# A hybrid encoder layer on one core: seven parts in the second feed-forward product, two stage-2 weight blocks prepared early, operand splits and loads re-timed

## The chip, the core and the metric

The kernel runs on one core of a Trainium2 chip. Its engines are TensorE (PE; its weight loads are shown as PEld), VectorE (DVE), ScalarE (ACT), GpSimd (POOL) and SyncE (SP), which issues nearly all DMAs. Each engine works through its own queue in order. The metric is the device time of one execution in microseconds; before the change it is 2453.44 us, the median of 3 runs (2451.5 to 2454.14).

## What is computed

One encoder layer on 2048 + 256 positions of width 1024, in float32, with a final norm:

```python
h = rmsnorm(x, norm1_g)
q, k, v, g, lr, u, vs, xp = split(h @ w_in)
a_out = gla_mixer(q, k, v, g, lr, ...)        # 512 channels, two directions, chunks of 64
b_out = spatial_gating(gelu(u), gelu(vs), ...) # 256 channels, chunks of 128
c_out = pool_mixer(xp, pool_w, pool_scale)     # 256 channels, windows 2, 4, 8, 16
x = x + concat([a_out, b_out, c_out]) @ w_o
h = rmsnorm(x, norm2_g)
a, up = split(h @ w1)                          # 2816 channels each
a = shift(a, -1) * cw[0] + a * cw[1] + shift(a, 1) * cw[2] + cb
x = x + (silu(a) * up) @ w2
y = rmsnorm(x, norm_f)
```

## The kernel before

Every large product works on float32 values split into a rounded high part and the rest: `split` copies the high part on ACT and subtracts it on DVE, or on POOL where it is told so. `mm3` then issues three matmuls (high times high, high times low, low times high). One such triple, followed by a call of `pipe.tick()`, is the unit of the schedule, a tick.

**How order is set.** TensorE's order is written out by hand. The other work stands in Python generators that are put into a `Pipe`, a heap of due ticks: `pipe.add(gen, d)` starts one d ticks from now, each `yield d` puts off its next piece by d ticks, and `tick()` emits what is due. An engine then runs its instructions in the order in which they were emitted, each waiting for its inputs and for its output buffer. From the second tile of stage 2 on, DVE, ACT, POOL and SP keep that order too; before it (stage 1 and the first tile of stage 2) a planner orders them.

**Stages.** Stage 1 runs 18 tiles of 128 positions through the first 1312 columns of `w_in` (weight tiles `wk0` to `wk7`) and computes the chunk sums of the gated attention in `post1`. Stage 2 runs the tiles again, in reverse order in five groups, through the other 1024 columns (`vk0` to `vk7`; raw blocks come through four `rawb` buffers, `w2prep` splits one). After each group `out2` does the product with `w_o`, adds `x`, and stores it in DRAM (`d_x`); `stat2` sums its squares with a matmul `pn`. The last group's `out2` runs at the start of the feed-forward part, with the operands of the first block being split beside it (`hprep`).

**Feed-forward.** Three blocks of two halves of 384 positions (halves 0 and 1). For each of 22 hidden columns `ffn1` computes both halves with seven half-depth products instead of eight, by sums of operands. The weight side (A11, S1, S2, S3, S4, A12, A22) is made by `operands()`, one operand per product, three products ahead (`astep` at the first triple of each). In block 0 it loads A22, A21, A11, A12 and makes S1 to S4 on POOL (`comb`), and `keep` stores them in DRAM for blocks 1 and 2. Raw operands share a ring of NR = 9 buffers; in blocks 1 and 2 they are loaded ND = 7 ahead. The activation side is eight arrays in four tiles: p = 0 holds B11 and B21, p = 1 holds T3 and B22, p = 2 holds T1 and T2, p = 3 holds T4. Their products come in the order B11, T1, T2, T3, B22, B21, T4. `bmake` makes these sums for the next block and stores them in DRAM; `bload` reads and splits them for the next block while the last part of this one runs (p = 0 and 2 on DVE, p = 1 and 3 on POOL), starting 30 ticks after the last hidden column begins, each piece 3 ticks after the one before.

A column has 28 ticks. `gate` then makes the gated hidden values, split into `uh` and `ul`. `ffn2` multiplies the columns of a part (`PARTS`) with the second weights, for eight output columns c and both halves, and adds the result into `x2`. One such c is a job: its raw weights come through `rg` (NRG = 3 buffers), `prepw2` splits them into `gh` and `gl` (2 buffers each), two jobs ahead of loads. One hidden column beyond the part is computed before the part's `ffn2` starts, except in the last part, where none is left: there the last column's values are the newest, and `late` puts them behind the others for the first c. In the last part `sqadd` also squares the new x on ACT and adds the squares into `acc` on POOL. `finish` turns them into the final norm: a matmul `pn`, a power on POOL, a matmul `pr`, eight multiplications on DVE, two stores, and then the loads of the next block's x (`load2f`). For half 0 of the last block `last_norm` does the same in another order.

## Time and profile before

| what | us |
|---|---|
| median of 3 runs | 2453.44 |
| the profiled execution | 2454.75 |
| its span | 2453.0 |
| stage 1 | about 0 to 372 |
| stage 2 and the product with `w_o` | about 372 to 840 |
| feed-forward block 0 | about 839 to 1382 |
| feed-forward block 1 | about 1382 to 1912 |
| feed-forward block 2 and the tail | about 1912 to 2453 |

The profile is one execution. Starts are counted from the start of its span. A row of the list of instructions gives the start, the time taken, engine, line, operation, output and inputs, and in brackets how long the engine stood idle before it and what released it. A row of waits gives the engine and the line that waited, what it waited for, the total, how often, and the longest. Matmuls are pipelined, so each takes about twice the distance to the next. The busy times of rows that are merged (x2, x4) run from the first start to the last end.

### The profile page before, as it was taken

To read this page: it belongs to the slowest core of one execution; us is meant where nothing else is said; L and a number is where in the kernel's file an instruction comes from. 1 tells how busy PE (TensorE), PEld (TensorE's weight loads), DVE (VectorE), ACT (ScalarE), POOL (GpSimd) and SP (SyncE) were. 2 spreads that over 40 slices of the span, in tenths; PEclk is the share of its full clock that TensorE was granted. 3 is DMA by queue.
4 is the path that set the end of the run, shared out by engine and by line. 5 is a ranking of instruction groups with operands and counts; after the bars stand their busy time and mean duration, and the time that the engine had idled before them with its cause. 6 is when DMAs were issued, how large, how long until landed. Compare 5 with 4: busy or idle time off the path is not lost.

```text
span 2453.0 us, 36854 instructions
## 1 busy us (share of the span) xinstructions
PE 2382.1 (97%) x13280; PEld 2268.6 (92%) x13280; DVE 1679.3 (68%) x2981; ACT 1034.4 (42%) x1928; POOL 794.2 (32%) x748
## 2 busy tenths in 40 slices
PE   8999998999999889999999899999999999999997
PEld 7899996988988789999999899999999999999997
DVE  6766657676666786777777686666677766666666
ACT  6444445333333443333334544433345533344334
POOL 3332221111011664455444622323223521222122
PEclk9999999999999999999999999999999999999998
DMA  6333224565664754454535464444434543333222
GB/s 202 136 129 112 78 73 150 173 191 149 205 191 128 221 164 128 136 171 155 159 104 160 142 223 118 145 134 126 127 102 155 181 138 100 103 112 104 92 94 87
DMA packets 227771, 343.51 MB, mean 140 GB/s; under 512 B 25634, under 2 KB 124962, under 8 KB 227588
## 3 DMA queue, kind: packets, MB, share of 16 engines
q1 hardware_dynamic: 220564, 318.21, 41.7%
q0 software_dynamic: 6752, 22.55, 2.4%
q8 instruction: 105, 1.72, 0.3%
q14 instruction: 78, 0.64, 0.1%
q10 hardware_dynamic: 272, 0.39, 0.0%
HBM read 261.81 MB, written 79.25 MB: 139 GB/s over the span
## 4 chain that ended last, share of the span: by engine, by line
PE 53%; DVE 4%; issue 3%; POOL 3%; DMA 1%; ACT 1%; SPq 0%; DVEq 0%; POOLq 0%; ACTq 0%
PE py L171 7%; PE py L170 6%; PE py L169 6%; PE fD L1158 3%; PE fA L1160 3%; PE fD L1159 3%; PE fA L1158 3%; PE fD L1160 3%; PE fA L1159 3%; PE fB L1158 2%; PE fB L1160 2%; PE fB L1159 2%; PE fC L1158 2%; PE fC L1160 2%; PE fC L1159 2%
## 5 line engine op out<-in xcount | busy, mean ns | idle before, releaser
L162 POOL TENSOR_TENSOR S<-S,S 128x512 fp32r<-128x512 f32 x242 | 329.7, 1363 | 757.5 <-ACT S L161 724.1
L171 PE MATMUL py<-uh,gl 128*128 128x384 f32 (+1 forms) x1056 | 359.2, 340 | 6.8 <-DVE gl L1225 6.7
L169 PE MATMUL py<-uh,gh 128*128 128x384 f32 (+1 forms) x1056 | 359.6, 341 | 3.2 <-ACT gh L1223 3.1
L170 PE MATMUL py<-ul,gh 128*128 128x384 f32 (+1 forms) x1056 | 358.9, 340 | 3.7 <-DVE ul L1188 3.7
L1270 DVE TENSOR_TENSOR x<-py,x 128x384 f32<-128x384 f32 (+1 forms) x384 | 213.1, 556 | 159.3 <-PE py L171 157.6
L162 DVE TENSOR_TENSOR A<-A,A 128x512 fp32r<-128x512 f32 x198 | 158.0, 798 | 178.5 <-ACT A L161 169.9
L161 ACT ACTIVATE A<-A 128x512 fp32r<-128x512 f32 x198 | 124.4, 630 | 218.8 <-issue 71.0
L171 PEld LDWEIGHTS py<-uh,gl 128*128 128x128 f32 x1056 | 200.1, 190 | 10.4 <-DVE gl L1225 10.4
L161 ACT ACTIVATE S<-S 128x512 fp32r<-128x512 f32 x242 | 152.2, 629 | 135.3 <-PE fE L1160 62.1
L170 PEld LDWEIGHTS py<-ul,gh 128*128 128x128 f32 x1056 | 200.1, 190 | 5.7 <-DVE ul L1188 5.3
L169 PEld LDWEIGHTS py<-uh,gh 128*128 128x128 f32 x1056 | 200.2, 190 | 4.8 <-ACT gh L1223 4.4
L1223 ACT ACTIVATE gh<-rg 128x384 fp32r<-128x384 f32 (+1 forms) x198 | 97.4, 493 | 223.8 <-PE py L170 207.0
L1158 PE MATMUL fA<-B,A 128*128 128x386 f32 (+1 forms) x528 | 180.2, 341 | 0.0
L1160 PE MATMUL fA<-B,A 128*128 128x386 f32 (+1 forms) x528 | 179.3, 339 | 0.0
L1159 PE MATMUL fA<-B,A 128*128 128x386 f32 (+1 forms) x528 | 178.6, 338 | 0.0
L169 PE MATMUL pm<-wk,xh 128*128 128x512 f32 (+2 forms) x432 | 166.4, 385 | 7.0 <-ACT wk L164 6.7
L170 PE MATMUL pm<-wk,xh 128*128 128x512 f32 (+2 forms) x432 | 157.0, 363 | 0.4 <-DVE wk L165 0.3
L171 PE MATMUL pm<-wk,xl 128*128 128x512 f32 (+2 forms) x432 | 156.2, 362 | 0.6 <-DVE xl L162 0.6
L1225 DVE TENSOR_TENSOR gl<-rg,gh 128x384 fp32r<-128x384 f32 (+1 forms) x198 | 119.4, 603 | 8.0 <-ACT gh L1223 8.0
L171 PE MATMUL pw<-mh,ol 128*128 128x512 f32 (+1 forms) x320 | 118.7, 371 | 2.9 <-DVE ol L162 2.9
L169 PE MATMUL qm<-vk,xh 128*128 128x512 f32 x288 | 118.9, 413 | 2.2 <-ACT vk L164 2.2
L169 PE MATMUL pw<-mh,oh 128*128 128x512 f32 (+1 forms) x320 | 118.4, 370 | 0.0
(279 smaller groups left out, 6223.2 us busy)
## 6 DMA issues: line engine op xcount, KB each, us to landing
A<-in_w SPq DMA_DIRECT2D x242, 256.0 KB, 3.7
S<-ds_S SPq DMA_DIRECT2D x176, 256.0 KB, 2.7
rg<-in_w SPq DMA_DIRECT2D x150, 192.0 KB, 2.7
xt<-in_xT SPq DMA_DIRECT2D x35, 512.0 KB, 4.3
ds_S<-S SPq DMA_DIRECT2D x66, 256.0 KB, 2.1
rawo<-dw SPq DMA_DIRECT2D x64, 256.0 KB, 4.4
dx<-xr SPq DMA_DIRECT2D x24, 256.0 KB, 2.5
rg<-in_w SPq DMA_DIRECT2D x48, 128.0 KB, 2.3
```

What stands on the lines that cost most here:

```text
L161: SC.activation(hi, src, AF.Copy)
L162: (eng or V).tensor_tensor(out=lo, in0=src, in1=hi.bitcast(F32), op=ALU.subtract)
L169: TE.matmul(out, lh, rhs_h, start=first, stop=False)
L170: TE.matmul(out, lh, rhs_l, start=False, stop=False)
L171: TE.matmul(out, ll, rhs_h, start=False, stop=last)
L1158: TE.matmul(o, ah, bh, start=st, stop=False, skip_group_check=True)
L1159: TE.matmul(o, ah, bl, start=False, stop=False, skip_group_check=True)
L1160: TE.matmul(o, al, bh, start=False, stop=kk == 3, skip_group_check=True)
L1223: SC.activation(gh[:, 0:n], rv, AF.Copy)
L1225: V.tensor_tensor(out=gl[:, 0:n], in0=rv, in1=gh[:, 0:n].bitcast(F32), op=ALU.subtract)
L1270: V.tensor_tensor(out=x2[:, c, 1:1 + no], in0=py[q][:, 0:no], in1=x2[:, c, 1:1 + no], op=ALU.add)
```

## The change

It makes these edits; the numbers in a schedule are ticks.

- `PARTS`: seven parts, six of three columns and one of four, instead of eight (five of three, two of two, one of three). `NU` becomes 4; `uh` and `ul` stay at 8 buffers (`NUT`).
- In the last part the jobs c = 0 and c = 1 are issued as one list (`late`): of c = 0 first the three older columns of half 1, then of half 0, then the newest column of half 1, all of c = 1 for half 1, the newest of half 0 for c = 0, and all of c = 1 for half 0. Job 2's weights are split at the end of c = 0, and job 4's are loaded at the end of the list.
- `bload` follows a table, `BORDER`: T1 and T2 (p = 2) at 13 to 22, within the last hidden column; p = 0 and p = 1 at 42 to 68; p = 3 at 78 to 90. Three loads are under way instead of four.
- `finish` starts 14 and 36 ticks after the last part instead of 2 and 28. The last norm's matmuls and diagonals come ahead of what is left of the other half's `finish` (`pipe.flush()` is moved), and all its diagonals are made on ACT.
- The first block's x is loaded from the schedule, 30 and 60 ticks after the feed-forward part begins (`first_x`), not at once. `stat2` of the last group comes 16 instead of 8 ticks after its products.
- `vk0` and `vk1` get a pool of their own (`vx`), allocated ahead of stage 1's weights; they are split during tiles 15 and 16, and their `rawb` buffers then load blocks 4 and 5. At the start of stage 2, blocks 2, 3 and 4 are split, and 5, 6 and 7 during its first three triples' worth of k.
- Rings: NR 9 to 8, ND 7 to 6, NRG 3 to 2, NZ 2 to 1 (stage 1's zeroed attention buffers). In `operands`, S3's sum is made one step earlier and the load of the next A11 goes out one step later, behind the store of S4. The load of `rg` for three jobs ahead is issued at a job's fifth triple instead of the third.

```diff
-NR = 9
-ND = 7
+NR = 8
+ND = 6
-NRG = 3
+NRG = 2
+NVX = 2
-HL = (1, 2)
+XG = 30
+BORDER = ((0, 2, 13), (1, 2, 16), (2, 2, 19), (3, 2, 22), (0, 0, 42), (0, 1, 45), (1, 0, 48), (1, 1, 52),
+          (2, 0, 56), (2, 1, 60), (3, 0, 64), (3, 1, 68), (0, 3, 78), (1, 3, 82), (2, 3, 86), (3, 3, 90))
-PARTS = (3, 3, 3, 3, 3, 2, 2, 3)
+PARTS = (3, 3, 3, 3, 3, 3, 4)
+NUT = 8
...
+    vx = pool("vx", 1)
+    vk = [vx.tile([P, 2, W2C], F32R, name=f"vk{k}") for k in range(NVX)]
+    def w2prep(k):
+        split(vk[k][:, 0], vk[k][:, 1], pre[k], vc[:, V_G1 + k:V_G1 + k + 1])
+        if k + NRAW < KD:
+            wbload(k + NRAW)
...
-        NZ = 2
+        NZ = 1
...
+            if NT - 1 - NVX <= i < NT - 1:
+                pipe.add(w2early(i - NT + 1 + NVX), 12)
...
-                        if g and k + 3 < KD:
-                            w2prep(k + 3)
+                        if g and k + NVX + 3 < KD:
+                            w2prep(k + NVX + 3)
...
-            pipe.add(stat2(u, acc, alloc), 8)
+            pipe.add(stat2(u, acc, alloc), 16 if between else 8)
...
-        for k in range(3):
+        for k in range(NVX, NVX + 3):
             w2prep(k)
-            if k == EV:
+            if k == NVX:
                 end1()
...
-            for p, _ in PAIRS:
-                load(0, p)
-            yield box["wait"]
-            for kk in range(4):
-                for p, eng in PAIRS:
...
+            for kk, p in todo[:NX - 1]:
+                load(kk, p)
+            at = 0
+            for n, (kk, p, tick) in enumerate(BORDER):
+                if tick > at:
+                    yield tick - at
+                    at = tick
+                m = 2 if p < 3 else 1
+                hi, src = B[p][:, 0, 0:m, kk, 0:w], got.pop((kk, p))
+                SC.activation(hi, src, AF.Copy)
+                yield 1
+                (GP if p % 2 else V).tensor_tensor(out=B[p][:, 1, 0:m, kk, 0:w], in0=src, in1=hi.bitcast(F32), op=ALU.subtract)
+                yield 1
+                at += 2
+                if n + NX - 1 < len(todo):
+                    load(*todo[n + NX - 1])
...
                 s2 = comb(rawt4("S2"), s1, a11, ALU.subtract)
+                s3 = comb(a21, a11, a21, ALU.subtract)
                 yield
                 operand(j, "S1", s1)
                 keep(j, "S1", s1)
-                s3 = comb(a21, a11, a21, ALU.subtract)
...
                 operand(j, "S4", s4)
-                if more:
-                    a11 = rawop(j + 1, "A11")
-                else:
+                if not more:
                     ahead(2)
                 yield
                 operand(j, "A12", a12)
                 keep(j, "S4", s4)
-                if not more:
+                if more:
+                    a11 = rawop(j + 1, "A11")
+                else:
                     ahead(2)
...
             if late:
-                order = [o for o in order if o[1] < n - 1] + [o for o in order if o[1] == n - 1]
+                a, b = range(n - 1), range(n)
+                order = [(t, q, k) for t, q, ks in ((0, 1, a), (0, 0, a), (0, 1, b[-1:]), (1, 1, b), (0, 0, b[-1:]), (1, 0, b))
+                         for k in ks]
...
+                if late:
+                    if (t, q, k) == (0, 0, n - 1):
+                        begin(prepw2(jobs[2]))
+                    if at == len(order) - 1:
+                        loadw2(jobs[4])
+                elif t and at == 0 and t + 1 < len(jobs):
                     begin(prepw2(jobs[t + 1]))
-                if at == 2 and 1 <= t and t + 3 < len(jobs):
+                elif t and at == min(4, len(order) - 1) and t + 3 < len(jobs):
                     loadw2(jobs[t + 3])
...
-                o, i, sc = dg[:, b * P:b * P + n], ident[:, P - n:P], r[:, b:b + 1]
-                if b % 2:
-                    SC.activation(o, i, AF.Copy, scale=sc)
-                else:
-                    V.tensor_scalar(out=o, in0=i, scalar1=sc, scalar2=None, op0=ALU.mult)
+                SC.activation(dg[:, b * P:b * P + n], ident[:, P - n:P], AF.Copy, scale=r[:, b:b + 1])
+            pipe.flush()
             TE.matmul(pr, ones, dg, start=True, stop=True)
...
-        xs = {q: load2f(segs, q, box["w"]) for q, segs in enumerate(BLOCKS[0])}
+        xs = {}
+        def first_x(w):
+            for q, segs in enumerate(BLOCKS[0]):
+                xs[q] = load2f(segs, q, w)
+                yield XG
+        pipe.add(first_x(box["w"]), XG)
...
-                    ffn2(jobs, t, sel if t or not lastq else (1, 0), xs, us, no, accs, final, lastq and not t)
+                    if not lastq or t > 1:
+                        ffn2(jobs, [(t, sel)], xs, us, no, accs, final)
+                    elif t == 0:
+                        ffn2(jobs, [(0, (1, 0)), (1, (1, 0))], xs, us, no, accs, final, True)
...
-                    pipe.add(finish(blk, q, xs, no, accs[q][0], FG, nxt), 2 + 26 * q)
+                    pipe.add(finish(blk, q, xs, no, accs[q][0], FG, nxt), 14 + 22 * q)
```

## The prediction

> **What bounds the kernel now.** I read the page's first part, then a table of stages, then who made TensorE wait.

> ```profile
> span 2453.0 us, 36854 instructions
> PE 2382.1 (97%) x13280; PEld 2268.6 (92%) x13280; DVE 1679.3 (68%) x2981; ACT 1034.4 (42%) x1928; POOL 794.2 (32%) x748
> ...
> 360.00:425.00 65.00, 55.05 (x285) 44.10 (x284) 44.62 (x105) 28.96 (x43) 9.74 (x15) 0.95 0.40 127
> ...
> 800.00:870.00 70.00, 57.00 (x254) 48.80 (x253) 51.22 (x63) 30.29 (x65) 46.42 (x40) 0.90 0.67 212
> 870.00:1335.00 465.00, 456.94 (x2576) 452.16 (x2575) 352.50 (x507) 182.58 (x347) 238.67 (x172) 1.00 0.45 142
> 1335.00:1410.00 75.00, 67.28 (x356) 65.53 (x354) 53.00 (x76) 42.61 (x80) 48.19 (x35) 0.93 0.55 169
> 1410.00:1865.00 455.00, 455.00 (x2582) 454.17 (x2583) 304.13 (x519) 183.96 (x347) 121.45 (x112) 1.00 0.44 137
> 1865.00:1925.00 60.00, 54.71 (x282) 52.81 (x282) 40.33 (x60) 35.00 (x66) 40.31 (x30) 0.91 0.53 168
> ```

> The stage rows give length, then busy time of PE, weight loads, DVE, ACT, POOL, then the granted clock. TensorE bounds the kernel: in 1410 to 1865 it is busy for all 455 us. Its matmuls there come every 455/2582 = 0.176 us, so three of them (one step of the schedule, a tick) take 0.53 us, one hidden column (84) 14.8 us, and a part of the second product of three columns (144) 25.4 us, of four (192) 33.8 us. The change removes no matmul. Time can only come from idle TensorE and from its slow clock. Idle is length less PE busy; the slow clock costs at most length times (1 - clock):

> - stage 1 to 2 (360 to 425): 9.9 idle, 3.2 slow
> - mixing to feed-forward (800 to 870): 13.0 and 7.0
> - first block (870 to 1335): 8.1 and 0
> - border of blocks 0 and 1 (1335 to 1410): 7.7 and 5.2
> - border of blocks 1 and 2 (1865 to 1925): 5.3 and 5.4

> That is 65 us, beside the tail. Who ended the waits, over the whole run:

> ```profile
> PE fD L1158 <- DVE u L1167: 10.4, 3, 8.4
> ...
> PE py L171 <- DVE gl L1225: 6.7, 9, 1.6
> PE pn L1290 <- POOL acc L1244: 5.7, 2, 4.3
> PE py L170 <- DVE ul L1188: 3.7, 3, 2.0
> ...
> PE qm L170 <- DVE vk L165: 2.4, 4, 0.8
> PE qm L169 <- ACT vk L164: 2.2, 3, 1.1
> ```

> (Total, times, longest.) All six lie where the change works.

> **Early stage-2 weights.** Stage 2 waits 2.4 + 2.2 = 4.6 us for its weights.

> ```profile
> L165 DVE SCALAR_TENSOR_TENSOR vk<-rawb,vc,vk 128x1024 fp32r<-128x1024 f32 x7 | 8.8, 1281 | 3.6 <-ACT vk L164 3.6
> ...
> 372.50:400.50 28.00, 22.43 (x97) 16.29 (x95) 22.93 (x49) 19.26 (x27) 1.98 (x3) 0.94 0.55 173
> ```

> Two of eight splits move into tiles 15 and 16, and their buffers fetch blocks 4 and 5 early, so the last weights are fetched sooner. But DVE is busy 22.93 of 28 us here, also with tile 17's chain; what leaves it is two splits of 1.28 us. I take that, 2.6 us, and 1.4 of the 3.6 us in which DVE waited for weights: **4.0 us**. At best all 4.6 us and 1.9 of slow clock go (6.5). At worst the splits (1.15 on ACT, 1.28 on DVE, twice) delay stage 1, whose order outside TensorE a planner sets, and 1 us is lost. One zeroed buffer pair less (NZ) costs nothing: a tile's pair is read right after it is written, one tile ahead of the next.

> **Late loads of x.** This is the largest wait.

> ```profile
> 844.74 6.72 SPq L924 DMA_DIRECT2D x<-dx  x4
> 851.50 0.66 SPq L1070 DMA_DIRECT2D ds_S<-A  x1
> 852.21 2.51 SPq L1065 DMA_DIRECT2D A<-in_w  x4
> ...
> 861.38 0.63 ACT L161 ACTIVATE A<-A 128x512 fp32r<-128x512 f32 x1 [11.94 <-DMA A<-in_w]
> ...
> 850.00:870.00 20.00, 11.64 (x53) 11.35 (x52) 7.69 (x12) 5.33 (x8) 8.86 (x8) 0.74 0.72 225
> ```

> SP's queue issues four x loads, 3.1 MB, ahead of column 0's A22: that is issued 7.5 us late and lands 9 us later, ACT waits, DVE's add stands behind the split, TensorE is idle 8.4 us and then slow. Now the x loads go out at ticks 30 and 60, first needed at tick 112. A22 goes out at about 845.4, lands after the usual 3.7 us at 849.1, and is split by 851; TensorE wants it at 854.7 (where its idle time began). Gain: the 8.4 us idle. Of the stretch's slow clock, 20 x 0.26 = 5.2 us, about half lies in the idle time; 1.8 us is kept as gain: **10.2 us**. The pn wait just ahead (1.8 us, for the last square sum, which the 16 ticks clear) gives nothing: S3's and S4's splits follow that same late work and are ready only as TensorE comes to them now. Bounds 6 (these two splits, and x in the A loads' way in columns 1 and 2) and 12.

> **Seven parts, smaller rings.** The two parts of two columns in block 0 (1255 to 1312) have four waits for gh and gl:

> ```profile
> PE py L171 <- DVE gl L1225: 1.4, 2, 0.7
> PE py L169 <- ACT gh L1223: 0.9, 2, 0.5
> ...
> A<-in_w SPq DMA_DIRECT2D x242, 256.0 KB, 3.7
> ...
> rg<-in_w SPq DMA_DIRECT2D x150, 192.0 KB, 2.7
> ```

> Together 2.3 us. One part of three takes their place; the run's other seven gl waits are 6.7 - 1.4 = 5.3 us, 0.8 each, so it keeps 0.8: **1.5 us**. The 48 adds into x that go lie beside matmuls. Two raw buffers for the second weights instead of three: a load can go out when DVE has split the one two jobs earlier, some 1.5 us into a job of 3.2 us, and is wanted 4.8 us later, against 2.7 to land: covered, up to 0.5 us a time if DVE lags. Bounds: 3 lost to 2.5 gained. Prefetch 6 instead of 7 is 12.7 us ahead of use: covered.

> **The borders.** Last column and last part of block 1, and POOL's groups of the first border:

> ```profile
> 1871.50:1884.30 12.80, 11.42 (x65) 10.94 (x63) 10.09 (x17) 7.01 (x13) 2.71 (x2) 1.00 0.37 114
> ...
> 1358.66 0.95 DVE L1050 TENSOR_TENSOR B<-b,B 128x772 fp32r<-128x772 f32 x1
> ...
> 1364.12 1.75 DVE L1050 TENSOR_TENSOR B<-b,B 128x772 fp32r<-128x772 f32 x1
> ...
> L1244 POOL TENSOR_TENSOR acc<-acc,sq 128x384 f32<-128x384 f32 x14 | 18.5, 1340 | 0.0
> L1050 POOL TENSOR_TENSOR B<-b,B 128x772 fp32r<-128x772 f32 x4 | 8.8, 2190 | 5.8 <-ACT B L1048 5.8
> L162 POOL TENSOR_TENSOR S<-S,S 128x512 fp32r<-128x512 f32 x5 | 6.4, 1280 | 8.9 <-ACT S L161 6.1 <-DMA rg<-in_w 2.8
> L1050 POOL TENSOR_TENSOR B<-b,B 128x386 fp32r<-128x386 f32 x4 | 4.8, 1196 | 0.0
> ```

> POOL's sums and splits take 18.5 + 8.8 + 4.8 = 32.1 us in a part of 25.4 us; POOL ends late, and pn waits for it. With four columns the part lasts 33.8 us and pn comes 20 instead of 8 ticks after it: 10.6 us more of room. The pn waits (4.3 and 1.4) go, and with them ACT's waits for POOL, behind which gh stands. What stays is the wait for ul. T1's and T2's four splits move into the last column's ticks 14 to 24, on a DVE busy 10.09 of 12.8 us: 4 x 0.95 = 3.8 us against 2.7 free, 1.1 late. The order of the products covers that: the newest of half 1 is wanted after six instead of four triples, 2 x 0.53 = 1.05 us later. So a ul wait like today's stays (2.0 and 1.4), with a slow stretch worth 1.7 us. First border: 7.7 + 5.2 - 2.0 - 1.7 - 1.2 (gl and pr) = **8.0 us**; second 5.3 + 5.4 - 1.4 - 1.7 - 0.6 = **7.0 us**. Bounds 2.5 and 11 each.

> [...]

> The slow clock follows waits as short as 2.0 us here: after the ul wait the next matmuls lie 0.32 us apart.

> ```profile
> 1357.53 0.52 PE L169 MATMUL py<-uh,gh 128*128 128x384 f32 x1
> 1357.85 0.52 PE L170 MATMUL py<-ul,gh 128*128 128x384 f32 x1
> ```

> [...]

> **The tail.** Six multiplications of the other half stand on DVE ahead of the last norm.

> ```profile
> 2436.14 3.27 DVE L1307 SCALAR_TENSOR_TENSOR x<-x,vc,acc 128x386 f32<-128x386 f32 x6
> ...
> 2436.83 1.05 PE L1334 MATMUL pm<-ones,sq 128*128 128x1 f32 x8
> ...
> 2440.88 0.59 ACT L1342 ACTIVATE acc<-ident,rt 128x128 f32<-128x128 f32 x2 [3.45 <-POOL rt L1337]
> ```

> They end at 2439.4; pm alone would allow 2437.9. Flushed later, they give 1.5 us, less 0.6 for four diagonals on ACT instead of two: **1.0 us** (0 to 2.5).

> **The sum.** 4.0 + 10.2 + 1.5 + 8.0 + 7.0 + 1.0 = 31.7 us. The profiled execution took 2454.75 us (span 2453.0), 1.3 above the median 2453.44; I take the sum from the median: 2421.7, **2422 us**. The raw load of A11, moved one step back, I cost at nothing: it is rival 3.

> **The rivals.**
> 1. *The last column becomes DVE's.* POOL splits S operands there, so T1's and T2's splits take 1.75 us each: 7.0 us, 4.3 late, 3.2 past the new order's cover. Each border then keeps that and one more slow stretch, some 4 us. For it: the last column has the fullest DVE. Against: POOL is busy only 2.71 of those 12.8 us. 2422 + 8 = **2430 us**.
> 2. *The borders are POOL's.* Its 32.1 us and S splits of 6.4 are 38.5 us; if they stretch further beside DVE, POOL ends late as now and the borders' 15 us stay: **2437 us**. Against: 33.8 + 10.6 us of room.
> 3. *Slower: A11 waits in block 0.* The A11 load now stands on SP behind the store of S4, which waits for POOL:

> ```profile
> 889.50 0.33 SPq L1070 DMA_DIRECT2D ds_S<-S  x1
> ...
> 893.29 1.50 POOL L1073 TENSOR_TENSOR S<-S,A 128x512 f32<-128x512 f32 x1
> 894.75 1.73 POOL L162 TENSOR_TENSOR S<-S,S 128x512 fp32r<-128x512 f32 x1
> ```

> Issued at 889.8, landed after 3.7 us at 893.5; then S2's and S3's sums and S1's split (1.5 + 1.7 + 1.7) end at 898.4, while the next column's S1 product comes at 900.7: 2.3 us in hand. From 6.0 us to land on, every microsecond costs 21 times. At 8 us it is 42 us: 2422 + 42 = **2464 us**. Only loads behind the x loads took that long.
> 4. *Nothing gained:* the removed waits come back one link further along the same queues: about **2451 us**.

> **Chances.** Forecast (2411 to 2428) 0.60; rival 1 0.20; rival 2 0.08; nothing gained 0.05; rival 3 0.07. Within 0.2% (4.9 us, about what a measurement of this kernel can tell from no change) is rival 4, slower is rival 3: faster 0.88, same 0.05, slower 0.07. The range 2410 to 2440 takes in the forecast and rivals 1 and 2.

> **What would show it.** The forecast: no fD wait over 1 us near 855 and no clock below 1 there; no pn wait on POOL at the borders; a ul wait of 1 to 2.5 us at each; no vk waits after stage 1. Wrong by rival 1: ul waits above 4 us. By rival 2: pn waits. By rival 3: waits of fC on S1's split in every column of block 0, its stage longer than 465 us less 1.5. A new wait in stage 1 would make the first term wrong.

## The result and the profile after

The changed kernel takes 2429.94 us (median of 4 runs, 2426.67 to 2433.09) against 2453.05 us for the kernel before (median of 4, 2451.50 to 2454.14): ratio 0.9908, 95% interval 0.9893 to 0.9923, 23 us or 0.9% less. The forecast was 2422 us with a range from 2410 to 2440; its terms sum to 31.7 us, 23 came.

The profiled execution took 2433.09 us, the longest of the four. Its page, first part:

```profile
span 2431.3 us, 36702 instructions
PE 2370.9 (98%) x13280; PEld 2260.7 (93%) x13280; DVE 1655.1 (68%) x2906; ACT 1032.7 (42%) x1905; POOL 791.4 (33%) x745
```

Both kernels issue the same 13280 matmuls. So the start of the n-th matmul can be compared in the two traces: how much earlier it starts after the change is the lead, and what the lead gains from one mark to the next is what that stage gave. The marks are times of the kernel before. The order differs at the norms' matmuls, which moved (near 845 and behind the borders), and in each block from the parts that changed their size to the end of the last part (1255 to 1351 in block 0). So at some marks, those of 1335 and 1865 above all, the n-th matmul is another one, and only the amount of work done by then is the same. Summed, the rows give the 21.7 us by which the spans differ (2453.0 less 2431.3).

| stage (time of before) | gain, us | forecast, us |
|---|---|---|
| 0 to 360, stage 1 | -0.5 | 0 |
| 360 to 425, stage 1 to 2 | 3.9 | 4.0 |
| 425 to 800, stage 2 | 0.8 | 0 |
| 800 to 870, mixing to feed-forward | 12.2 | 10.2 |
| 870 to 915.4, columns 1 to 3 of block 0 | **-3.7** | 0 |
| 915.4 to 1335, rest of block 0 | **-1.5** | 1.5 |
| 1335 to 1410, border of blocks 0 and 1 | 7.2 | 8.0 |
| 1410 to 1465, columns after it | **-2.0** | 0 |
| 1465 to 1865, rest of block 1 | -0.3 | 0 |
| 1865 to 1925, border of blocks 1 and 2 | 6.7 | 7.0 |
| 1925 to 1990, columns after it | **-2.7** | 0 |
| 1990 to the end, with the tail | 1.6 | 1.0 |

The table of stages of the changed kernel, cut at the same matmuls (length, then busy time of PE, weight loads, DVE, ACT, POOL, then the granted clock):

```profile
360.60:421.70 61.10, 51.88 (x284) 43.05 (x283) 42.10 (x102) 26.99 (x40) 10.55 (x15) 0.97 0.38 118
795.90:853.70 57.80, 53.41 (x254) 45.22 (x253) 49.73 (x63) 30.02 (x64) 42.96 (x37) 1.00 0.65 205
853.70:902.90 49.20, 44.55 (x243) 42.05 (x243) 41.87 (x49) 22.23 (x44) 35.80 (x26) 1.00 0.65 210
902.90:1323.90 421.00, 414.51 (x2334) 411.47 (x2333) 307.17 (x443) 164.00 (x307) 210.48 (x152) 1.00 0.46 146
1323.90:1391.80 67.90, 64.33 (x357) 63.48 (x356) 48.31 (x65) 38.86 (x71) 41.65 (x32) 0.97 0.49 155
1391.80:1448.70 56.90, 54.95 (x311) 54.02 (x310) 47.83 (x79) 25.58 (x51) 15.27 (x11) 1.00 0.67 219
...
1848.90:1902.30 53.40, 51.33 (x284) 50.91 (x283) 37.00 (x49) 30.48 (x54) 35.04 (x26) 0.97 0.46 144
1902.30:1970.10 67.80, 65.30 (x369) 64.15 (x368) 55.07 (x89) 31.89 (x63) 21.68 (x20) 1.00 0.64 201
```

The kernel before had TensorE busy for 43.3 of 45.4 us in columns 1 to 3, and without a break after the borders:

```profile
870.00:915.40 45.40, 43.31 (x243) 42.28 (x242) 40.03 (x48) 21.81 (x43) 34.24 (x24) 1.00 0.54 170
915.40:1335.00 419.60, 413.63 (x2335) 409.89 (x2334) 312.47 (x459) 160.78 (x306) 204.43 (x148) 1.00 0.44 139
```
```profile
1410.00:1465.00 55.00, 55.00 (x312) 54.73 (x313) 48.06 (x78) 25.68 (x51) 16.28 (x12) 1.00 0.75 241
1925.00:1990.00 65.00, 65.00 (x369) 64.47 (x368) 56.44 (x89) 32.33 (x61) 21.59 (x19) 1.00 0.68 212
```

So the gains are where they were looked for, and four stages that were forecast at no loss or a small gain give back 9.9 us: the bold rows. The waits of TensorE over the whole run name the instructions:

```profile
PE fD L1173 <- DVE u L1182: 8.0, 6, 2.2
...
PE py L174 <- DVE gl L1240: 5.5, 7, 2.2
PE py L173 <- DVE ul L1203: 4.1, 2, 2.1
```

No pn wait on POOL is left, nor one for `vk`. The one wait of 8.4 us for `u` is gone, and there are six of at most 2.2 us: 3.4 us in columns 1 to 3, 0.9 later in block 0, 3.7 behind the two borders. `u` is DVE's sum behind the product with S3, the fourth of a column (u3), and the column's last product, into the same bank fD, waits until that sum has read it.

### The profile page after: what moved, and what is told of

It is laid out like the page before. It is cut to its first block, busy times and chain, and to the rows that moved or that the text cites. A ratio compares the mean times of both kernels' runs of the same rounds, so it can differ in the third digit from the quotient of the medians.

```text
span 2431.3 us, 36702 instructions
## 1 busy us (share of the span) xinstructions
PE 2370.9 (98%) x13280; PEld 2260.7 (93%) x13280; DVE 1655.1 (68%) x2906; ACT 1032.7 (42%) x1905; POOL 791.4 (33%) x745
## 4 chain that ended last, share of the span: by engine, by line
PE 84%; DVE 6%; issue 3%; POOL 3%; DMA 2%; ACT 2%; SPq 0%; DVEq 0%; POOLq 0%; ACTq 0%
PE py L174 7%; PE py L173 7%; PE py L172 7%; PE pm L172 3%; PE pm L173 3%; PE pm L174 3%; PE fA L1175 3%; PE fA L1173 3%; PE fA L1174 3%; PE fD L1173 3%; PE fD L1175 3%; PE fD L1174 3%; PE qm L172 2%; PE qm L174 2%; PE qm L173 2%
## 5 line engine op out<-in xcount | busy, mean ns | idle before, releaser
L165 POOL TENSOR_TENSOR S<-S,S 128x512 fp32r<-128x512 f32 x242 | 327.0, 1352 | 726.1 <-ACT S L164 660.3
L1294 DVE TENSOR_TENSOR x<-py,x 128x384 f32<-128x384 f32 (+1 forms) x336 | 187.2, 557 | 187.1 <-PE py L174 185.8
L165 DVE TENSOR_TENSOR A<-A,A 128x512 fp32r<-128x512 f32 x198 | 170.9, 863 | 167.2 <-ACT A L164 147.1
L164 ACT ACTIVATE A<-A 128x512 fp32r<-128x512 f32 x198 | 124.9, 631 | 215.0 <-issue 81.9
L164 ACT ACTIVATE S<-S 128x512 fp32r<-128x512 f32 x242 | 151.9, 628 | 134.0 <-PE fE L1175 65.1
## 6 DMA issues: line engine op xcount, KB each, us to landing
A<-in_w SPq DMA_DIRECT2D x242, 256.0 KB, 3.7
S<-ds_S SPq DMA_DIRECT2D x176, 256.0 KB, 2.7
rg<-in_w SPq DMA_DIRECT2D x144, 192.0 KB, 2.5
ds_S<-S SPq DMA_DIRECT2D x66, 256.0 KB, 2.1
rawo<-dw SPq DMA_DIRECT2D x64, 256.0 KB, 4.6
rg<-in_w SPq DMA_DIRECT2D x30, 256.0 KB, 2.7
dx<-xr SPq DMA_DIRECT2D x24, 256.0 KB, 2.5
```

Of the source, the lines that this page charges most:

```text
L164: SC.activation(hi, src, AF.Copy)
L165: (eng or V).tensor_tensor(out=lo, in0=src, in1=hi.bitcast(F32), op=ALU.subtract)
L1294: V.tensor_tensor(out=x2[:, c, 1:1 + no], in0=py[t, q][:, 0:no], in1=x2[:, c, 1:1 + no], op=ALU.add)
```

## The experiments

Five questions were open: whether the late A11 load or the x loads cost columns 1 to 3 their time (or a third thing); what cost the rest of block 0; what the columns after the borders wait for; what makes the ul wait; and whether a better version exists.

| kernel | median, us | ratio to before, 95% |
|---|---|---|
| a1 old operand order | 2430.71 | 0.9887 to 0.9920 |
| a2 x in eight pieces | 2431.84 | 0.9894 to 0.9924 |
| a3 old second product | 2443.62 | 0.9943 to 0.9972 |
| a4 norm at its old places | 2427.15 | 0.9879 to 0.9908 |
| b1 before + late x | 2449.28 | 0.9975 to 0.9994 |
| b2 before + new operand order | 2457.92 | 1.0011 to 1.0032 |
| b3 x at ticks 84 and 98 | 2424.69 | 0.9870 to 0.9903 |
| b4 b3 + a4 + old order from column 4 | 2423.36 | 0.9862 to 0.9891 |
| c1 T1, T2 splits in the last part | 2427.98 | 0.9883 to 0.9912 |
| c2 b4 + c1 | 2424.68 | 0.9871 to 0.9901 |
| c3 b3 without the shifted terms, columns 0 to 2 | 2423.18 | 0.9863 to 0.9896 |
| d1 b4 with the splits spread | 2422.42 | 0.9852 to 0.9885 |

Many of these intervals overlap with that of the changed kernel, so an effect of a few us is read from the length of its stage, not from the totals. Two stages of block 0, cut at the same counts of matmuls in every trace, one trace for each kernel:

| | columns 1 to 3 | rest of block 0 |
|---|---|---|
| before (x first, old order, eight parts) | 45.4 | 419.6 |
| b2 (x first, new order, eight parts) | 50.0 | 422.5 |
| b1 (x late, old order, eight parts) | 51.7 | 418.3 |
| a3 (x late, new order, eight parts) | 48.4 | 425.2 |
| changed kernel (x late, new order, seven parts) | 49.2 | 421.0 |
| a1 (x late, old order, seven parts) | 51.0 | 416.1 |
| a2 (as changed, x in pieces) | 49.4 | 419.4 |
| b3 (as changed, x at 84 and 98) | 48.8 | 418.4 |
| c3 (b3, less work on DVE) | 43.0 | 419.4 |
| b4 (b3, old order from column 4) | 48.4 | 416.1 |

These lengths scatter too. The kernels a4 and c1 below have the changed kernel's code in both stages, and their traces show 49.4 and 50.2 us, then 419.5 and 419.8. A difference of 1.5 us between two traces is therefore no effect by itself.

### a1: the old operand order

```diff
                 s2 = comb(rawt4("S2"), s1, a11, ALU.subtract)
-                s3 = comb(a21, a11, a21, ALU.subtract)
                 yield
...
                 keep(j, "S1", s1)
+                s3 = comb(a21, a11, a21, ALU.subtract)
...
                 operand(j, "S4", s4)
-                if not more:
+                if more:
+                    a11 = rawop(j + 1, "A11")
+                else:
                     ahead(2)
...
```

> The changed kernel with the old order inside the weight operands alone: the next column's A11 is loaded one step earlier, ahead of the store of S4, and S3's sum is made one step later; the raw ring stays at 8. Theory A (the late A11 load costs block 0 its 3.7 us between 857 and 901): the waits of fD and fE on the operand adds and on S3's split at 878, 883 and 900 shrink from 4.6 us to under 1.5, the lead over the kernel before holds at 14 us or more at the first part of the second product (12.7 now), total 2426 to 2428. Theory X (the x loads in the transfer queue are the cause): these waits stay above 3.5 us, total 2429 to 2431. Theory R (the ring of 8 needs the late load): new waits of SP for a raw buffer, every column of block 0 loses some 0.2 us or more, total above 2432.

Columns 1 to 3 became longer (51.0 against 49.2 us), the rest of block 0 shorter (416.1 against 421.0), and the total stayed. Theory A, which put the loss of columns 1 to 3 on the late A11, falls. One sign of theory R appears: SP stood for 4 us in one A load, waiting for one of the eight buffers.

```profile
859.18 4.07 SPq L1080 DMA_DIRECT2D A<-in_w  x1
```

It is not the cause: b1, with nine buffers, has no such wait and is as long there (51.7 us), and the loss in every column and the total above 2432 us that theory R expected did not come. Past column 3 the old order is the better one by 4.9 us, which no theory had: the wait for `u` is gone and the `gl` waits there fall from 4.8 to 3.0 us. This lies beyond the scatter: the four traces with the old order from column 4 on and seven parts (a1, b4, c2, d1) take 414.9 to 416.1 us there, the six with the new order (the changed kernel, a2, a4, b3, c1, c3) 418.4 to 421.0.

### a2: x in eight pieces, and b3: x late enough to be out of the way

```diff
-                xs[q] = load2f(segs, q, w)
-                yield XG
...
+                for k in range(0, KD, 2):
+                    load_cols(x2[:, k:k + 2], segs, slice(k, k + 2), d_x)
+                    yield 10
```

> The changed kernel with the first block's x loaded in eight pieces of two of eight rows-blocks each, 10 ticks apart from tick 30 to 100, instead of two pieces at 30 and 60. Theory X: no A operand waits for more than about 1.2 us behind a piece (4.3 and 2.7 us now), the waits at 878 and 883 (1.9 us) go and that at 900 (2.0 us) shrinks, lead at the first part of the second product 15 us or more (12.7 now), total 2426 to 2428. Theory A: the piece matters little, the waits stay above 3 us, total 2429 to 2431.

The first waits went, that for `u` at the end of column 3 stayed, and the stage kept its length (49.4 us). Some A splits still stood 2 to 3 us for loads, so this alone did not settle it; b3 moves the x loads away:

```diff
-                yield XG
+                yield 14
...
-        pipe.add(first_x(box["w"]), XG)
+        pipe.add(first_x(box["w"]), 84)
```

> The changed kernel with the first block's x loaded at ticks 84 and 98 instead of 30 and 60, so that no x load stands beside the operands of columns 0 to 2; the first add into x comes at tick 115. Theory X: the loss of 3.7 us between column 1's start and the first part shrinks to 1.5 or less, A's splits wait less than 1 us for their loads, total 2426 to 2428. Theory C: A's splits wait less, but the waits of fD and fE in columns 1 to 3 stay at 3 us or more in sum, because DVE's and GpSimd's own queues are what is late; total 2429 to 2432. If x lands late for its first add: a wait of the second part's products behind DVE, total above 2432.

With no x load beside columns 0 to 2 the stage is still 48.8 us long, 3.4 more than before, and the waits for `u` sum to 3.2 us. Theory X falls as the cause; theory C is left. A splits still wait for their own loads (6.1 us in all, 2.4 at most), so the loads remain a rival to DVE's and POOL's queues until c3. The total of 2424.69 us is lower than either theory had. In the trace b3 ends 10.7 us ahead of the changed kernel: 3.4 us of that are there at 845 already and 3.3 arise at the first border, in code that this edit does not touch.

### b1 and b2: one part alone on the kernel before

```diff
-        xs = {q: load2f(segs, q, box["w"]) for q, segs in enumerate(BLOCKS[0])}
...
+        pipe.add(first_x(box["w"]), 30)
...
-            pipe.add(stat2(u, acc, alloc), 8)
+            pipe.add(stat2(u, acc, alloc), 16 if between else 8)
```

> The kernel before with one part of the change alone: the first block's x loaded from the schedule at ticks 30 and 60, and the last group's square sums 16 ticks after its products; the operands keep their old order and a ring of 9. Theory C (columns 0 to 3 run at the pace of the operands' chain, which starts without a lead in either kernel, so that most of a wait taken away ahead of them comes back inside them): the lead rises by 10 us or more to column 1's start and falls by 3 to 4.5 us until the first part of the second product; 6.5 to 8.5 us stay to the end; total 2445 to 2447. Theory A (the loss there comes from the new order and the smaller rings of the changed kernel): no loss over 1 us in columns 1 to 3, 10 us stay, total 2442 to 2444.

The lead rose by 9.7 us up to column 1 (from 2.4 at 845 to 12.1) and fell by 6.3 until the first part. Of the total 3.4 us are left (ratio 0.9985, 0.9975 to 0.9994). Theory C was right on the mechanism, and too mild: with the old order and a ring of 9 more comes back than in the changed kernel, and the total lies above its 2445 to 2447 us. The operands show the missing lead. In the kernel before, the split of each S operand of column 1 ends 1.0 to 2.9 us ahead of the operand's first product; in b1 two of the four end up to 0.8 us behind it, and the other two 0.7 us ahead.

For b2 the operand order of the change was put into the kernel before, rings as they were (the diff of a1 backwards).

> The kernel before with one part alone: the new order inside the weight operands (A11's load behind the store of S4, S3's sum one step earlier), with the rings as before (9 and 7). Theory A2 (the new order costs 3 to 5 us in columns 4 to 21 of block 0, by columns in which A11's split comes late and the splits behind it fall in beside GpSimd's sums): the lead falls by 2 to 5 us between the first part and the last of block 0, total 2455 to 2458. Prediction as it stood (nothing): within 1 us, total 2453 to 2454.

It is slower by 0.2% (1.0011 to 1.0032): 4.6 us in columns 1 to 3 and 2.9 in the rest of the block. Theory A2 is right on the rest of the block and the total, the forecast's "nothing" wrong; the loss in columns 1 to 3 it did not have. Of those 4.6 us, 2.1 had been gained just ahead, where the wait for `u` is 4.0 us instead of 8.4: a shorter stop is followed by a longer stage here too. With x late the new order is 1.8 us shorter in columns 1 to 3 than the old one (49.2 against 51.0), hardly more than the scatter. In the rest of the block it costs 2 to 7 us in every pairing (418.3 and 419.6 against 422.5 and 425.2 with eight parts, 416.1 against 418.4 to 421.0 with seven).

### c3: less work on DVE

```diff
-                V.scalar_tensor_tensor(out=t0, in0=a[:, 0:no], scalar=cw(0), in1=t0, op0=ALU.mult, op1=ALU.add)
-                V.scalar_tensor_tensor(out=t0, in0=a[:, 2:2 + no], scalar=cw(2), in1=t0, op0=ALU.mult, op1=ALU.add)
+                if i > 2:
+                    V.scalar_tensor_tensor(out=t0, in0=a[:, 0:no], scalar=cw(0), in1=t0, op0=ALU.mult, op1=ALU.add)
+                    V.scalar_tensor_tensor(out=t0, in0=a[:, 2:2 + no], scalar=cw(2), in1=t0, op0=ALU.mult, op1=ALU.add)
```

> The version with x at ticks 84 and 98, with the two shifted terms of the convolution left out in hidden columns 0 to 2 of block 0 (four DVE instructions less per column, 0.62 to 1.6 us each). Theory C with DVE as the late queue: the waits in columns 1 to 3, 3.3 us of lead lost between column 1's start and the first part, fall to 1.5 us or less, and the slack of the S4 operand (-0.5 us) rises above 0. Theory C with GpSimd or the loads as what is late: the slack of S3 and S4 in columns 1 to 3 and the loss stay within 0.7 us of what they are.

This kernel leaves two terms of the convolution out of three columns, so it shows only where the time goes. It settles columns 1 to 3. The first fence is b3, the second c3, the same matmuls:

```profile
850.40:899.20 48.80, 45.45 (x243) 43.56 (x243) 42.60 (x50) 22.72 (x44) 36.94 (x27) 0.97 0.67 213
```
```profile
853.60:896.60 43.00, 42.78 (x243) 42.49 (x243) 36.30 (x40) 22.59 (x43) 36.14 (x26) 1.00 0.73 231
```

Ten DVE instructions fewer, 6.3 us of DVE's time, and the stage is 5.8 us shorter, with TensorE busy for all but 0.2 us; POOL and the loads did as much as before, and ACT waited as long for A loads (5.9 us against 6.1), so neither the loads nor the amount of POOL's work was what held TensorE up. Whether the time of these DVE instructions counts or their meetings with POOL's was not tried apart. The operand S4 is ready 1.3 to 1.9 us ahead of its product in columns 2 and 3 (c3) instead of half a microsecond behind its first matmul, which needs only the high part (b3). DVE's queue in the changed kernel shows how it comes about at the end of column 3:

```profile
896.91 0.56 DVE L1182 TENSOR_TENSOR e<-fC,e 128x386 f32<-128x386 f32 x1
897.39 0.97 DVE L165 TENSOR_TENSOR A<-A,A 128x512 fp32r<-128x512 f32 x1
898.27 1.61 DVE L1240 TENSOR_TENSOR gl<-rg,gh 128x384 fp32r<-128x384 f32 x1
899.81 0.55 DVE L1182 TENSOR_TENSOR u<-fD,e 128x386 f32<-128x386 f32 x1
```

`u` stands behind a split of weights that took 1.61 us, all of it beside POOL's work:

```profile
897.76 1.72 POOL L1088 TENSOR_TENSOR A<-A,A 128x512 f32<-128x512 f32 x1
899.44 1.59 POOL L165 TENSOR_TENSOR S<-S,S 128x512 fp32r<-128x512 f32 x1
```

In c3 the same instruction took 0.55 us, as did in the changed kernel the 99 of these splits of 128x384 that ran with POOL idle (0.54 to 0.56 us). Of the 45 that met POOL's work most took as little (median 0.55), the longest 1.65 us.

### a3: the old second product

`PARTS = (3, 3, 3, 3, 3, 2, 2, 3)`, `NRG = 3`, and the load of `rg` at a job's third triple, in the changed kernel.

> The changed kernel with the old second product's sizes: eight parts (3,3,3,3,3,2,2,3), three raw buffers for the second weights, their load at a job's third triple. Theory N (two raw buffers cost block 0 its gl waits): the gl and gh waits after the first columns of block 0, some 5.5 us with the slow stretch at 1128, fall to the 4 us or less of the kernel before, no slow clock near 1128; but the two parts of two columns bring back 2.3 us and the last part of 25 us brings POOL's pn waits back at the borders (2 to 5 us each). Total 2430 to 2436. If the seven parts gave what was forecast (1.5 us) and the ring nothing: gl waits as now, total 2432 to 2438, with the borders the larger part of it.

The cost is 13.7 us of the total, which at 2443.62 us lies above the ranges of both theories. The rest of block 0 is 4.2 us longer (425.2 against 421.0), so seven parts with two raw buffers are worth 4.2 us, 2.2 with the old order (418.3 in b1 against 416.1 in a1, whose ring of raw operands differs too) or 3.5 against the kernel before; the forecast had 1.5. The borders lose too: 70.3 against 67.9 us and 57.6 against 53.4. Its gl waits in block 0 sum to 6.4 us, not fewer than with two raw buffers (4.8), so theory N is not borne out. Nor do the pn waits on POOL come back at the borders, as both theories had it: none is left. What stands there instead are gl and gh waits, 2.6 us in sum at each border.

### a4: the final norm at its old places

```diff
-                    pipe.add(finish(blk, q, xs, no, accs[q][0], FG, nxt), 14 + 22 * q)
+                    pipe.add(finish(blk, q, xs, no, accs[q][0], FG, nxt), 2 + 26 * q)
```

> The changed kernel with the final norm of blocks 0 and 1 at its old places, 2 and 28 ticks after the last part instead of 14 and 36. Theory F (the new places put half 1's x load just ahead of the next part's second weights): the waits near 1433 and 1955 (2.8 and 3.4 us) go, and pn waits on POOL at the borders stay under 0.5 us because the part of four columns gives the room, total 2423 to 2426. Rival: POOL still ends late and the 12 ticks were what cleared pn; pn waits of 1 to 4 us come back at each border, total 2428 to 2434.

Theory F holds. From the first border to the columns after the second, a4's TensorE waits are

```profile
PE py L173 <- DVE ul L1203: 4.1, 2, 2.1
PE pn L1314 <- POOL acc L1259: 1.3, 2, 0.7
PE py L174 <- DVE gl L1240: 0.3, 1, 0.3
```

where the changed kernel, in the same stretch, has the same 4.1 us for ul, 1.5 for uh, 0.8 for gl, and

```profile
PE fD L1173 <- DVE u L1182: 3.7, 2, 2.2
```

The columns after the borders run nearly as in the kernel before (55.5 and 65.1 us; 56.9 and 67.8 in the changed kernel):

```profile
1390.40:1445.90 55.50, 55.18 (x312) 54.59 (x312) 48.01 (x78) 25.69 (x50) 16.31 (x12) 1.00 0.72 234
1898.50:1963.60 65.10, 65.10 (x368) 64.57 (x367) 56.44 (x89) 32.33 (x61) 21.53 (x19) 1.00 0.66 209
```

The total, 2427.15 us, is 1 us above theory F's range, and its interval overlaps with that of the changed kernel. The chain in the changed kernel, on SP and then on ACT and DVE:

```profile
1422.36 1.24 SPq L936 DMA_DIRECT2D x<-dx  x2
1423.65 1.08 SPq L1080 DMA_DIRECT2D S<-ds_S  x1
1424.78 1.12 SPq L1231 DMA_DIRECT2D rg<-in_w  x2
```
```profile
1431.18 0.52 ACT L1238 ACTIVATE gh<-rg 128x384 fp32r<-128x384 f32 x1 [4.44 <-DMA rg<-in_w]
```
```profile
1431.73 0.56 DVE L1240 TENSOR_TENSOR gl<-rg,gh 128x384 fp32r<-128x384 f32 x1 [2.40 <-ACT gh L1238]
1432.21 0.55 DVE L1182 TENSOR_TENSOR u<-fD,e 128x386 f32<-128x386 f32 x1
```

The norm is later, so half 1's x load goes out at 1422.4 just ahead of the next part's raw weights. Their split starts 6.4 us after the issue, where such a load takes 2.5 in the median of the run:

```profile
rg<-in_w SPq DMA_DIRECT2D x144, 192.0 KB, 2.5
```

So ACT stands in `gh`, DVE in `gl`, and `u`, which needs neither, stands behind. In a4 the x load goes out at 1416.9 and the rg loads at 1421.3. The pn waits that the later place was to clear are 0.6 and 0.7 us in a4: the part of four columns had nearly cleared them already. In a3 the later place alone, with a part of three columns, left none; so each of the two edits does most of it by itself.

### c1: the T1 and T2 splits out of the last column

```diff
-BORDER = ((0, 2, 13), (1, 2, 16), (2, 2, 19), (3, 2, 22), (0, 0, 42), (0, 1, 45), (1, 0, 48), (1, 1, 52),
-          (2, 0, 56), (2, 1, 60), (3, 0, 64), (3, 1, 68), (0, 3, 78), (1, 3, 82), (2, 3, 86), (3, 3, 90))
+BORDER = ((0, 2, 40), (1, 2, 43), (2, 2, 46), (3, 2, 49), (0, 0, 53), (0, 1, 56), (1, 0, 59), (1, 1, 62),
+          (2, 0, 65), (2, 1, 68), (3, 0, 71), (3, 1, 74), (0, 3, 78), (1, 3, 82), (2, 3, 86), (3, 3, 90))
```

> The changed kernel with the next block's T1 and T2 splits taken out of the last hidden column: they follow at ticks 40 to 49, and the pieces of B11, B21, T3 and B22 at 53 to 74, all within the last part; the four-column part and the order with the newest products late stay. Theory T (the wait for the last column's ul, 2.1 us and a slow stretch of 1.7 us at each border, comes from these four splits on DVE ahead of the gate; block 2 has none of them and no such wait): ul and uh waits under 0.5 us at both borders, no slow clock near 1340 and 1862, 5 to 7 us gained in all, total 2423 to 2425. Prediction as it stood (the later place of the newest products covers the splits, the wait is the gate's own): ul waits as now within 0.5 us. Rival: the part becomes too full for DVE or GpSimd, gl or pn waits of 2 us or more at each border, total 2429 to 2433.

The waits at the first border, changed kernel and then c1:

```profile
PE py L173 <- DVE ul L1203: 2.1, 1, 2.1
PE py L172 <- ACT uh L1201: 1.5, 1, 1.5
```
```profile
PE py L174 <- DVE gl L1240: 1.3, 2, 1.1
PE py L173 <- DVE ul L1203: 0.5, 1, 0.5
```

Theory T holds for the waits: ul falls to 0.5, uh goes, and the clock is 1.00 in both borders, which are 64.7 and 52.2 us long against 67.9 and 53.4:

```profile
1322.20:1386.90 64.70, 62.88 (x355) 61.66 (x354) 46.59 (x63) 38.13 (x70) 42.12 (x31) 1.00 0.52 161
1843.80:1896.00 52.20, 50.17 (x283) 49.23 (x283) 37.39 (x49) 30.58 (x54) 35.97 (x26) 1.00 0.46 144
```

In the changed kernel DVE had three of those splits around the column's last sum, ahead of the end of its gate:

```profile
1329.56 2.06 DVE L1064 TENSOR_TENSOR B<-b,B 128x772 fp32r<-128x772 f32 x1
1331.54 0.55 DVE L1182 TENSOR_TENSOR e<-fE,e 128x386 f32<-128x386 f32 x1
1332.01 0.95 DVE L1064 TENSOR_TENSOR B<-b,B 128x772 fp32r<-128x772 f32 x1
...
1334.66 0.95 DVE L1064 TENSOR_TENSOR B<-b,B 128x772 fp32r<-128x772 f32 x1
```

The rival has a share: gl waits of 1.1 us come up in the fuller part. Of the 5 to 7 us expected 4.4 appear at the borders, and even these are not shown to be the edit's: b3 has the changed kernel's code there and its ul wait of 2.1 us, but no slow clock at the first border, which took 64.6 us. The total came down by 2.0 us, within the intervals, and fits neither theory's range.

### b4, c2 and d1: a better version

b4 puts x at 84 and 98, the norm at 2 and 28, and the old order from column 4 on (`if j < 4` around the new places of S3's sum and A11's load).

> The changed kernel with three edits together: x at ticks 84 and 98, the final norm at its old places (2 and 28), and the old order of the operands from column 4 on (the new one in columns 0 to 3). By the runs so far: 5 us from the norm's places, 4 to 5 us from the order in columns 4 to 21, 0 to 2.5 us from x: total 2418 to 2422. If the gains share waits: 2423 to 2426.

c2 adds c1's table.

> The version with x at ticks 84 and 98, the norm at its old places and the old operand order from column 4 on (2423.4 us), with the T1 and T2 splits in the last part as well. Theory T: 5 to 7 us less, total 2416 to 2419. If the norm at its old places needs the room that the splits now take: pn waits of 1 to 4 us at each border, total 2420 to 2424.

d1 spreads the T1 and T2 splits between the others (p = 0, 2, 1 for each depth, from 42 to 78, then p = 3 to 90) and puts the norm at 7 and 31.

> The version with x at ticks 84 and 98 and the old operand order from column 4 on, with the four T1 and T2 splits spread over the last part between those of B11 and B21 (one piece every three to four ticks from 42 to 90) and the norm at 7 and 31 ticks. If DVE's and GpSimd's queues in the last part were only too dense: no ul wait over 0.6 us, no pn wait over 0.5 us, gl waits of 0.5 us or less and no slow stretch at both borders, total 2416 to 2420. If the part is full whatever the order: gl or pn waits of 1 us or more at each border, total 2421 to 2425, no better than the version with the splits in the last column (2423.4).

b4 took 2423.36 us, 29 less than before and within the range for gains that share waits; its block 0 is as hoped (48.4 and 416.1 us) and the columns after its borders lose 0.3 us and nothing. In c2 the pn waits grow from b4's 0.6 and 0.8 us to 1.5 at each border (the first):

```profile
PE py L174 <- DVE gl L1245: 1.8, 2, 1.1
PE pn L1319 <- POOL acc L1264: 1.5, 1, 1.5
```

Its total, 2424.68 us, is 0.7 us above the range of its second theory. Spread out, the pn waits are 0.2 us, but other waits take their place (d1, first border and the columns after it):

```profile
PE py L173 <- DVE ul L1208: 1.6, 1, 1.6
PE py L174 <- DVE gl L1245: 1.4, 2, 1.1
PE fD L1178 <- DVE u L1187: 1.3, 2, 1.0
PE pn L1319 <- POOL acc L1264: 0.2, 1, 0.2
```

The part is full whatever the order, as the second theory had it. d1's 2422.42 us (ratio 0.9869, 0.9852 to 0.9885) is the lowest of the versions that compute everything; it cannot be told from b4 or c2. Its interval lies below that of the changed kernel (0.9893 to 0.9923), so it is the faster one, as is b4 (0.9862 to 0.9891); by how much, 2 us or 10, the runs leave open.

## Why the prediction was right, and where not

- **What bounds it**: right. The gains came from idle time and from slow clock, at the places named.
- **Early weights, 4.0**: 3.9 by the stage; the vk waits are gone. That the two figures agree so well is in part luck: b2, whose code is that of the kernel before there, was 2.5 us shorter than it in this stage. Which part of the gain DVE's moved splits gave was not tried alone.
- **Late x, 10.2**: the wait went and the stage gave 12.2 us, but columns 1 to 3 took back 3.7, so 8.5 stayed, inside the bounds of 6 to 12. Of the 12.2, 2.6 were gained by 845, ahead of the stop: the pn wait of 1.8 us stood there, whose removal the forecast counted as nothing (b2, which still has this wait, gained 0.7). The stop alone gave 9.6, near the forecast, of which 5.9 stayed; that the whole lies well inside the bounds is thanks to pn. The step that failed is the end of that part: I asked what is late next only for column 0's S3 and S4 and took the operands to follow. They do not: until the first second product DVE has 40 us of work in 45 (the row of 870 to 915.4), and a chain that starts without a lead never gets one. The stop of 8.4 us and the slow clock behind it had given it that lead (the splits of column 1 in the kernel before and in b1). My bound named x in the way of the A loads; b3 showed that it is not x, and c3 that it is DVE's queue.
- **Seven parts and smaller rings, 1.5, and A11 at nothing**: together -1.5. The parts were sized too low: 3.5 us against the kernel before, with the old order (a1). The A11 load "costed at nothing" and S3's sum took 4.9 of that back (a1 against the changed kernel; 2 to 6 by the other traces). Rival 3 had the right edit, but the wrong place: no fC wait in every column, only now and then a late `u` and `gl`. What exactly turns single columns late was not settled.
- **The borders, 8.0 and 7.0**: 7.2 and 6.7. No pn wait, a ul wait of 2.1 us and one slow stretch at each, as forecast; that one followed at both was luck, as the last section shows. The reason given for the ul wait was half wrong: the later place of the newest products would cover the gate; what it does not cover is the four splits in the last column (c1). The 1.7 us for a slow stretch are its length at half the clock: 3.41 us from 1356.74 in the kernel before. Rival 1 named those splits; its 1.75 us is the row at 1364.12, which ran beside POOL's `acc` sums, while those at 1356.85 and 1358.66, 0.96 and 0.95 us, had POOL idle. After the change the four took 0.96, 2.06, 0.95 and 0.95 us at the first border, the second beside POOL's S split at 1329.19 (1.60 us) and the others with POOL idle, so one of the four was slowed and not all, and they cost about what stands in the sum, not 4 us more.
- **The columns after the borders, nothing**: -2.0 and -2.7. This is the step with the largest error, and no rival held it. I counted the 12 ticks of `finish` as room for POOL and did not follow the DMAs which that generator issues at its end: the x loads, which it moved to just ahead of the rg loads (a4).
- **The tail, 1.0**: 1.6 with all that follows 1990.

Together: 1.7 too much for x, 3.0 for block 0's rest, 1.1 for the borders, 4.7 for the columns after them, against 0.5 too little in the rest: the 10.0 us by which the sum of 31.7 passes the 21.7 of the spans.

## What to carry to other kernels

A long wait can also be what gives the next work its lead: before it is booked as gain, count how full the queues of the engines that prepare that work are until the next stretch that needs little of them. When a piece of work is moved to a later tick, follow the loads which it issues last, not only the wait which it clears. An order of loads that is free beside one schedule can cost beside another: try it in both.

## What was not expected of the hardware

Waits of nearly the same length do not cost the same. In the changed kernel TensorE waited 2.2 us for `u` in the columns after the second border and the clock stayed at 1.00; in c1 the wait at the same place was 2.1 us and the clock fell.

```profile
1946.90:1950.30 3.40, 1.43 (x8) 1.46 (x9) 2.61 (x5) 2.45 (x5) 1.11 (x1) 1.00 1.02 375
1950.30:1953.70 3.40, 3.40 (x13) 3.40 (x12) 2.77 (x4) 1.44 (x4) 1.61 (x2) 0.50 0.48 160
```
```profile
1950.60:1954.00 3.40, 2.46 (x14) 2.13 (x13) 0.33 (x1) 0.52 (x2) 0.00 (x0) 1.00 1.07 392
1954.00:1957.40 3.40, 2.18 (x13) 2.22 (x14) 3.36 (x6) 2.68 (x6) 1.29 (x1) 1.00 0.85 308
```

Over all 14 traces, the first and last 20 us left out, each of the 38 full-speed windows in which TensorE was idle for 1.95 us or more was followed by a slow one, and none with less than 1.25 us idle was; between the two it came out both ways: in the kernel before a window with 1.43 us idle (from 1916.5) was followed by a slow one, and one with 1.60 us (from 1134.9) was not. A slow window costs some 1.5 us, an estimate from matmuls that come 0.32 us apart in it instead of 0.176. So the ul wait of 2.1 us at the borders cost that much more or not by where it fell: at both borders in the changed kernel, only at the second in b3, only at the first in a4 and b4.

One execution also differs from the next in code that is the same. Up to the end of stage 1 b3 and b4 have the same instructions as the changed kernel, yet b3's wait for `at` near the start was 1.2 us and b4's 2.3. At 360 b3 leads the kernel before by 0.6 us, and b4 lies 2.6 behind it. That is why totals that are 3 us apart say little here, and stages more.
